# One layer of a conditioned hybrid decoder: both heads of a pair scored in one step, the mask added to the gate row, SSD decay on ScalarE, the later modulation sums on VectorE

## The chip, the core and the metric

The kernel runs on one core of one Trainium2 chip. A core has TensorE (PE in the profile; PEld is its weight load), VectorE (DVE), ScalarE (ACT), GpSimd (POOL) and SyncE (SP), which here issues every DMA. The metric is device time in microseconds (us), the median of the timed runs.

## The reference, cut to what matters

One layer, batch 1, 1024 tokens, width 1024, all in float32:

```
mod = silu(c) @ w_ada + b_ada -> sh1, sc1, g1, sh2, sc2, g2
h   = x * (1 + sc1) + sh1 ;  proj = h @ w_in -> z | xBC | dt | q | k | v | f
SSD (16 heads of 64, chunks of 128):  conv + SiLU on xBC;  a_cs = cumsum(dt * A)
    scores[l,s] = (C B^T)[l,s] * exp(a_cs[l] - a_cs[s]) for s <= l, else 0;  y = scores @ x + carried state
FoX (16 heads of 64, blocks of 128 queries):  logit[t,s] = q_t . k_s / 8 + cum[t] - cum[s], s <= t
    softmax over s, times v          (cum: running sum of log forget gates)
y = concat @ w_out;  x = LN(alpha x + (1+g1) y)
h = x * (1 + sc2) + sh2;  x = LN(alpha x + (1+g2) (relu(h W1)^2 W2))
```

## The kernel before, in words

All large products are done as three matmuls of a high and a low part (`split`, L72 to L88: hi = rounded to fp32r, lo = rest; products hi·hi, hi·lo, lo·hi). Activations lie transposed, features on partitions and tokens on columns. The stages, in the order of time:

1. **h tiles** (L148): for each of 8 blocks of 128 features the sums for sc1 and sh1 (`ada_sum`, L128: 512 KB of `w_ada`, a GpSimd product, a VectorE reduction over k, then a matmul with ones), then h = x·(1+sc1)+sh1 and its split.
2. **SSD**, head pair by head pair (`ssd`, L380). Per pair the 24 matmuls of each half of a projection (`conv_tile`, `z_tile`), the chunk states, and the decay scores: GpSimd subtracts the pair's column of `cs` from the broadcast row `arow` (L414), VectorE takes the minimum with 0 (L415), ScalarE the Exp (L416), VectorE the product with C·B (L417); eight matmuls per head follow, all of one head, then all of the other. Their weights `xc` have 64 columns, so each head writes one half of the 128 output partitions: the profile calls the shape 128*64 (rows*columns of the array). They are true f32 products, of two MATMUL records each.
3. **Attention** in units (pair, g, head), g = 0 to 3, each of two blocks of 128 queries (`probs`, L490). q and k of a head are stored stacked, hi on its 64 partitions and lo on the other 64 (L468 to L475); `swap` (L523) makes a copy of q with the halves exchanged by DMA. So two matmuls that use all 128 rows give the four products, and a third, of bf16 constants, adds the causal mask in PSUM. VectorE adds the gate row `cum` and takes the maximum (L515), ScalarE does the Exp, GpSimd the division. `weigh` transposes the probabilities and multiplies with v.
4. Between the units a generator `fill` puts in the projections of the next pair and then the first half of the output projection; PIECES says how many pieces go where. `ada_some` puts in the later modulation sums (sc2, sh2, g2, g1: `ada_rest`, 32 steps), and `w2_sums` (L170, 14 calls in the attention loop) differences of blocks of the second MLP weight, on GpSimd through tile `w_b`.
5. Second half of the output projection, layer norm, and the two MLP products in a seven-product (Strassen) form.

The order on each engine is not the order of the text: the tile scheduler lists the instructions by a timing model of its own. A load may start as soon as its buffer is free, so `w2_sums`, written in the attention loop, stands far earlier in the program that is built. `with after(x)` keeps a load behind instruction x.

PSUM has tags `mm` (1 bank), `o` (1), `t` (2 buffers of one bank) and `S` (2 buffers of two banks).

Of the kernel before, what the change touches and what calls it, by code (L numbers as in the profile page):

```python
# [27 lines left out]
NEG = -1.0e30  # L28
# [4 lines left out]
def layer_kernel(ctx, tc, x, xT, cols, rows3, w_ada, b_ada, w_in, w_dtf, w_out, ln_rows, w1, w2, out):  # L33
# [59 lines left out]
    identb = cst.tile([P, P], BF16, name="identb")  # L93
    nc.vector.tensor_copy(identb, identf)
# [33 lines left out]
    def ada_sum(sec, j, tag, name):  # L128
# [4 lines left out]
        red = sb.tile([P, P], F32, name="ada_red", tag="q2", bufs=4)  # L133
# [39 lines left out]
    def w2_sums():  # L173
# [4 lines left out]
        load(t, w2r[:, :, n, :].rearrange("p i (h c) -> p i h c", h=2))  # L178
# [9 lines left out]
    def ada_rest(sec, j):  # L188
        red = ada_sum(sec, j, "raw", "r")
        yield  # L190
        pst = PT("mm", "adar_ps", (P, P))
        if sec in (G1, G2):
            mm(pst, ones, red, True, True)
            if j == 0:
                gsum[sec] = dr.tile([P, 1024], F32, name=f"grow{sec}")
            g = sb.tile([P, P], F32, name="ada_g", tag="q2", bufs=4)
            nc.vector.tensor_copy(g, pst)
            load(gsum[sec][:, j * P:(j + 1) * P], g)
        else:
            mm(pst[:, 0:1], red, ones[:, 0:1], True, True)  # L200
            nc.vector.tensor_tensor(mod_t[:, sec, j:j + 1], pst[:, 0:1], b_t[:, sec * 8 + j:sec * 8 + j + 1], op=ALU.add)

    rest = [(s, j) for s in (SC2, SH2, G2, G1) for j in range(8)]

    pend = []

    def ada_some(n):
        for g in pend:
            next(g, None)
        pend.clear()  # L210
        for _ in range(min(n, len(rest))):
            g = ada_rest(*rest.pop(0))
            next(g)
            pend.append(g)
# [104 lines left out]
    def forget_rows():
# [6 lines left out]
        row_form(16)  # L326
# [54 lines left out]
    def ssd(p, xs, z):  # L381
# [27 lines left out]
        ydg = PT("S", "s2_ps", (P, 8, P))  # L409
        for h in range(2):  # L410
# [37 lines left out]
    def qkv(p, st):  # L448
# [3 lines left out]
        for n, idx, scale in (("q", KI + p, 0.125), ("k", VI + p, 1.0), ("v", None, None)):  # L452
            w, _ = ws[-1]
            if idx is not None:
                ws.append(w_prep(w_in[idx]))
                marks["w"] = ws[-1][1]
                st[n] = ts = [R4("qk", f"{n}_st") for _ in range(2)]
# [3 lines left out]
            for half in range(2):  # L461
# [93 lines left out]
    def finish(p, g, o, yT):  # L555
# [687 lines left out]
```

## Time and profile before

| | |
|---|---|
| median of 3 runs | 1744.4 us (1743.99 to 1746.87) |
| the profiled execution | 1748.06 us, of which the span of the instructions is 1746.3 us |
| mean granted TensorE clock | 0.976 |
| busy: PE, PEld, DVE, ACT, POOL | 1661.9, 1382.3, 1290.3, 704.5, 889.5 us |
| chain that ended last | PE 70%, DVE 17%, issue 4%, POOL 3%, DMA 3%, ACT 3% |

The ends of matmuls in the profile are modelled: a record of 0.39 us may be followed by the next after 0.23 us, and only the distance from start to start says what a matmul costs in a stream. A row such as `x38` holds 38 merged instructions: first start, then the time to the end of the last. "f32" in a matmul row is the width of the words; it doesn't tell fp32r from float32.

### The profile page before, as it was taken

How to read it: one execution, taken by the hardware profiler on the slowest of the kernel's cores; microseconds unless marked ns; L12 is line 12 of the kernel's file. 1: busy time of each engine (PE TensorE's matmuls, PEld its weight loads, DVE VectorE, ACT ScalarE, POOL GpSimd, SP SyncE). 2: the span in 40 equal slices, each digit the busy share in tenths (PEclk: the TensorE clock that was granted, in tenths of full speed). 3: DMA queues.
4: the chain of work that ended last, by engine and by line, in shares of the span. 5: the costliest groups of instructions: out<-in, count | busy, mean ns of one | idle time of the engine just before them, and what ended most of it. 6: DMA issues, size and time to landing. Idle time of an engine off the chain costs nothing.

```text
span 1746.3 us, 22839 instructions
## 1 busy us (share of the span) xinstructions
PE 1661.9 (95%) x8316; PEld 1382.3 (79%) x8316; DVE 1290.3 (74%) x1914; ACT 704.5 (40%) x1189; POOL 889.5 (51%) x686
## 2 busy tenths in 40 slices
PE   7878899999999999999999999799999999999996
PEld 6667688888888888888778887688888878888885
DVE  6889878886777777776776478986767855746668
ACT  3235332322444544553665434633333334344322
POOL 5859863533544444442442445566656624704535
PEclk8989999999999999999999999899999999999998
DMA  9467764422223323222333744044434596666512
GB/s 373 149 210 258 246 217 137 151 79 77 96 84 115 103 85 117 90 66 63 109 123 113 237 157 169 37 164 144 145 137 160 175 342 208 248 243 205 193 37 96
DMA packets 112032, 268.72 MB, mean 154 GB/s; under 512 B 10128, under 2 KB 37008, under 8 KB 111920
## 3 DMA queue, kind: packets, MB, share of 16 engines
q1 hardware_dynamic: 111920, 267.27, 44.6%
q8 instruction: 65, 1.06, 0.2%
q14 instruction: 47, 0.39, 0.1%
HBM read 194.22 MB, written 64.62 MB: 148 GB/s over the span
## 4 chain that ended last, share of the span: by engine, by line
PE 70%; DVE 17%; issue 4%; POOL 3%; DMA 3%; ACT 3%; SPq 0%; DVEq 0%; ACTq 0%; POOLq 0%
PE mm_ps L62 25%; PE f_ps L953 15%; PE s_ps L1069 9%; PE y_ps L1069 7%; PE s_ps L62 6%; PE o_ps L62 4%; PE t_ps L542 3%; DVE conv_a L345 2%; DVE ada_red L134 1%; DVE w_hl L85 1%; POOL w_b L181 1%; DMA w_b<-in_w_dram 1%; DMA raw_w<-in_w_dram 1%; DVE h_hl L85 1%; DVE probs L515 1%
## 5 line engine op out<-in xcount | busy, mean ns | idle before, releaser
L62 PE MATMUL mm_ps<-h_hl,w_hl 128*128 128x512 f32 x2016 | 504.7, 400 | 8.1 <-DVE w_hl L85 5.2
L62 PEld LDWEIGHTS mm_ps<-h_hl,w_hl 128*128 128x128 f32 x2016 | 372.6, 191 | 83.6 <-DVE w_hl L85 7.1
L85 DVE TENSOR_TENSOR w_op<-raw_w,w_op 128x512 fp32r<-128x512 f32 (+1 forms) x149 | 188.2, 1268 | 22.9 <-ACT w_op L81 22.4
L953 PE MATMUL f_ps<-h_s,w_op 128*128 128x512 f32 x768 | 183.3, 393 | 6.2 <-ACT h_s L81 3.0
L520 POOL TENSOR_SCALAR probs<-probs,m 128x128 f32<-128x128 f32 (+7 forms) x128 | 101.9, 800 | 157.0 <-DVE m L519 137.7
L953 PEld LDWEIGHTS f_ps<-h_s,w_op 128*128 128x128 f32 x768 | 145.6, 190 | 38.0 <-ACT h_s L81 3.4
L81 ACT CAST w_op<-raw_w 128x512 fp32r<-128x512 f32 (+1 forms) x149 | 114.7, 775 | 100.7 <-PE f_ps L953 52.9
L1069 PE MATMUL s_ps<-w_op,a_op 128*128 128x512 f32 x672 | 153.7, 390 | 1.4 <-DVE a_op L85 1.1
L1069 PEld LDWEIGHTS s_ps<-w_op,a_op 128*128 128x128 f32 x672 | 125.9, 188 | 28.7 <-DVE a_op L85 1.6
L85 DVE TENSOR_TENSOR a_op<-a_ld,a_op 128x1024 fp32r<-128x1024 f32 x53 | 75.3, 1422 | 97.3 <-ACT a_op L81 97.3
L132 POOL TENSOR_TENSOR raw_ada<-raw_ada,c_act 128x1024 f32<-128x1024 f32 x44 | 94.8, 2162 | 99.0 <-DMA raw_ada<-in_w_ada_dram 82.4
L953 PE MATMUL f_ps<-h_hl,w_op 128*128 128x512 f32 x576 | 136.8, 389 | 0.0
L518 ACT ACTIVATE probs<-probs,m 128x128 f32<-128x128 f32 (+7 forms) x128 | 99.3, 776 | 90.9 <-DVE m L517 79.0
L953 PEld LDWEIGHTS f_ps<-h_hl,w_op 128*128 128x128 f32 x576 | 108.0, 188 | 22.4
L515 DVE CUSTOM_DVE_ANT_0 probs<-s_ps,cumrow 128x128 f32<-128x128 f32 (+7 forms) x128 | 95.1, 753 | 37.0 <-PE s_ps L62 23.2
L544 ACT CAST pt_hl<-t_ps 128x512 fp32r<-128x512 f32 (+1 forms) x160 | 84.6, 541 | 87.9 <-PE t_ps L542 85.6
L81 ACT CAST a_op<-a_ld 128x1024 fp32r<-128x1024 f32 x53 | 55.7, 1054 | 159.7 <-PE s_ps L1069 85.1
L545 DVE TENSOR_TENSOR pt_hl<-t_ps,pt_hl 128x512 fp32r<-128x512 f32 (+1 forms) x160 | 99.7, 632 | 21.2 <-ACT pt_hl L544 19.9
L62 PE MATMUL o_ps<-pt_hl,v_s 128*128 128x256 f32 (+1 forms) x640 | 111.8, 297 | 3.5 <-DVE m L517 1.5
L1069 PE MATMUL y_ps<-w_op,a_op 128*128 128x512 f32 x504 | 114.7, 389 | 0.0
L85 DVE TENSOR_TENSOR w_hl<-raw_w,w_hl 128x512 fp32r<-128x512 f32 x88 | 81.7, 937 | 39.5 <-POOL w_hl L79 39.3
L1069 PEld LDWEIGHTS y_ps<-w_op,a_op 128*128 128x128 f32 x504 | 94.6, 188 | 19.6
(255 smaller groups left out, 3214.1 us busy)
## 6 DMA issues: line engine op xcount, KB each, us to landing
raw_w<-in_w_dram SPq DMA_DIRECT2D x57, 512.0 KB, 4.1
a_ld<-ad SPq DMA_DIRECT2D x49, 512.0 KB, 4.4
raw_ada<-in_w_ada_dram SPq DMA_DIRECT2D x48, 512.0 KB, 4.0
raw_w<-in_w_in_dram SPq DMA_DIRECT2D x44, 512.0 KB, 3.8
w_b<-in_w_dram SPq DMA_DIRECT2D x14, 1024.0 KB, 7.5
w2t<-w_b SPq DMA_DIRECT2D x14, 1024.0 KB, 5.1
ad<-a_s SPq DMA_DIRECT2D x28, 512.0 KB, 3.3
raw_w<-w2t SPq DMA_DIRECT2D x28, 512.0 KB, 4.9
```

What stands on the lines that cost most here:

```text
L62: nc.tensor.matmul(o, l, r, start=start, stop=stop)
L81: nc.scalar.copy(hi, raw)
L85: eng.tensor_tensor(lo, raw, hi.bitcast(F32), op=ALU.subtract)
L132: nc.gpsimd.tensor_tensor(raw, raw, c_act.unsqueeze(2).broadcast_to([P, KT, P]), op=ALU.mult)
L515: nc.vector.tensor_tensor_reduce(out=pt, in0=sp[:, :W], in1=cum[:, :W], op0=ALU.add, op1=ALU.max, scale=1.0, scalar=-3.0e38, accum_out=m[: ...
L518: nc.scalar.activation(pt, pt, AF.Exp, bias=m[:, 1:2], scale=1.0, accum_out=m[:, 2:3])
L520: nc.gpsimd.tensor_scalar(pt, pt, m[:, 3:4], 1.0, op0=ALU.mult, op1=ALU.mult)
L542: nc.tensor.transpose(tp[:, at:at + P], pts[ti][:, s * P:(s + 1) * P], identf)
L544: nc.scalar.copy(hl[:, 0, :n], tp[:, :n])
L545: nc.vector.tensor_tensor(hl[:, 1, :n], tp[:, :n], hl[:, 0, :n].bitcast(F32), op=ALU.subtract)
L953: nc.tensor.matmul(o, l, r, start=first and k == 0 and m == 0, stop=last and k == 3 and m == 2, skip_group_check=True)
L1069: nc.tensor.matmul(banks[j], ahl[a_][:, n, js], whl[w_][:, n, :], start=first and d == 0 and n == 0 and m == 0, stop=last and d == ND - 1 ...
```

## The change

- **Scores of attention.** A unit is now (pair, g) with both heads. q and k of a pair are split into hi and lo tiles with one head on partitions 0 to 63 and the other on 64 to 127; `probs` does three products (hi·hi, hi·lo, lo·hi) per head on 64 rows of the array, written so that the heads alternate. The swapped copy, its DMAs and the stacking on GpSimd and VectorE are gone. g now runs 3, 2, 1, 0.
- **Mask.** No bf16 matmul: GpSimd adds the mask to the 128 diagonal columns of the gate row in place. The sign of q·k and of the row is turned, so that the minimum is taken, which serves the Exp directly as bias; the small negation on VectorE is gone.
- **SSD decay.** Subtraction and minimum become eight ScalarE Relus of 128 columns per head, with the column of `cs` as bias; the Exp takes scale -1. The eight matmuls of the two heads alternate.
- **Later modulation sums.** `w_adb` is laid out so that a load brings two k blocks of 512 columns; VectorE does one multiply-add over 512 columns per k block, in 32 steps of two, in place of GpSimd's product and VectorE's reduction. A matmul follows every four steps. g1 and g2 are kept as one row.
- **w2_sums** moves to the SSD loop, two calls per pair, and its load waits for a projection's weight load.

```diff
-    def ada_rest(sec, j):
-        red = ada_sum(sec, j, "raw", "r")
+    def ada_rest(sec, hg):
+        red = sb.tile([P, 512], F32, name="ada_sum", tag="ada", bufs=1)
+        for kp in range(4):
+            raw = T4("raw", "raw_adb", shape=(P, 2, 512))
+            load(raw, w_adb[((sec - 2) * 2 + hg) * 4 + kp])
+            for i in range(2):
+                c = c_act[:, 2 * kp + i:2 * kp + i + 1]
+                if kp == 0 and i == 0:
+                    nc.vector.tensor_scalar(red, raw[:, i, :], c, None, op0=ALU.mult)
+                else:
+                    nc.vector.scalar_tensor_tensor(red, raw[:, i, :], c, red, op0=ALU.mult, op1=ALU.add)
+            yield
...
-        load(t, w2r[:, :, n, :].rearrange("p i (h c) -> p i h c", h=2))
+        with after(marks["w"]):
+            load(t, w2r[:, :, n, :].rearrange("p i (h c) -> p i h c", h=2))
...
-            nc.gpsimd.tensor_tensor(sc, ar, cs[:, :, h0 + h:h0 + h + 1].broadcast_to([P, 8, P]), op=ALU.subtract)
-            nc.vector.tensor_scalar(sc, sc, 0.0, None, op0=ALU.min)
-            nc.scalar.activation(sc, sc, AF.Exp)
+            for b in range(8):
+                nc.scalar.activation(sc[:, b, :], ar[:, b, :], AF.Relu, bias=cs[:, b, h0 + h:h0 + h + 1], scale=-1.0)
+            nc.scalar.activation(sc, sc, AF.Exp, scale=-1.0)
             nc.vector.tensor_tensor(sc, sc, CBM[g], op=ALU.mult)
-            for b in range(8):
-                mm(ydg[h * 64:h * 64 + 64, b, :], xc[:, b, h, :], sc[:, b, :], True, True)
+            scs.append(sc)
+        for b in range(8):
+            for h in range(2):
+                mm(ydg[h * 64:h * 64 + 64, b, :], xc[:, b, h, :], scs[h][:, b, :], True, True)
...
-        wn = w_prep(w_in[XI + p + 1])[0]
+        wn, marks["w"] = w_prep(w_in[XI + p + 1])
         ssd(p, *xz[p])
+        for _ in range(2):
+            w2_sums()
...
-                    e = sm.tile([P, 512], F32, name="qk_e", tag="o_half", bufs=2)
-                    nc.scalar.activation(e, o, AF.Copy, scale=scale)
-                    for h in range(2):
...
-                        nc.gpsimd.tensor_scalar(t[mine, hs], e[mine, :], 1.0, 1.0, op0=ALU.mult, op1=ALU.mult)
-                        nc.vector.tensor_tensor(t[other, hs], e[mine, :], t[mine, hs].bitcast(F32), op=ALU.subtract)
+                    split(o, st[n][0][:, hs], st[n][1][:, hs], "act", scale=scale)
...
-                mm(sp[:, s0:s1], q1[:, tb * P:(tb + 1) * P], k[:, s0:s1], True, False)
-                mm(sp[:, s0:s1], q2[:, i * P:(i + 1) * P], k[:, s0:s1], False, not last)
-                if last:
-                    mm(sp[:, tb * P:W], identb, maskb, False, True)
+            for m, (a, b) in enumerate(((qh, kh), (qh, kl), (ql, kh))):
+                for h in range(2):
+                    hp = slice(h * 64, h * 64 + 64)
+                    mm(u["sp"][h][:, at + s0:at + s1], a[hp, tb * P:(tb + 1) * P], b[hp, s0:s1], m == 0, m == 2)
+        for h in range(2):
+            sp, pt, cum = u["sp"][h][:, at:at + W], u["pt"][h][:, at:at + W], cums[u["p"]][h]
+            nc.gpsimd.tensor_tensor(cum[:, tb * P:W], cum[:, tb * P:W], maskf, op=ALU.add)
...
-            if g in (1, 3) or p == 7:
-                ada_some(2)
-            if g in (0, 2) and p < 7:
-                w2_sums()
+        if g in (0, 2) or p == 7:
+            ada_some(2)
```

**Where the instructions go.** GpSimd in the h tiles: `raw_ada` are the products of stage 1, `w_hl` splits of projection weights, `w_b` the sums of the second MLP weight. Before:

```order
L132 TENSOR_TENSOR raw_ada<-raw_ada,c_act 128x1024 x8
L79 TENSOR_SCALAR w_hl<-raw_w 128x512
L181 TENSOR_TENSOR w_b<-w_b 128x512 x2
L132 TENSOR_TENSOR raw_ada<-raw_ada,c_act 128x1024
L79 TENSOR_SCALAR w_hl<-raw_w 128x512
L181 TENSOR_TENSOR w_b<-w_b 128x512 x2
L132 TENSOR_TENSOR raw_ada<-raw_ada,c_act 128x1024
L181 TENSOR_TENSOR w_b<-w_b 128x512 x2
```

The same place after the change:

```order
L128 TENSOR_TENSOR raw_ada<-raw_ada,c_act 128x1024 x8
L79 TENSOR_SCALAR w_hl<-raw_w 128x512
L128 TENSOR_TENSOR raw_ada<-raw_ada,c_act 128x1024 x2
L79 TENSOR_SCALAR w_hl<-raw_w 128x512
L128 TENSOR_TENSOR raw_ada<-raw_ada,c_act 128x1024 x2
L79 TENSOR_SCALAR w_hl<-raw_w 128x512 x3
L178 TENSOR_TENSOR w_b<-w_b 128x512 x2
L79 TENSOR_SCALAR w_hl<-raw_w 128x512
```

The `w_b` operations no longer stand between the products: 24 of the 56 stood ahead of the first pair's `xd` (L391), 9 do now.

PE in the SSD stage, the third pair's score matmuls (`scores_1385` and `scores_1400` are the two heads). Before:

```order
L62 MATMUL s2_ps_1354<-xd_1351,b_nat_545 128x128 x7
L62 MATMUL s2_ps_1382<-scores_1385,xc_1350 64x128 x8
L62 MATMUL s2_ps_1382<-scores_1400,xc_1350 64x128 x8
L62 MATMUL mm_ps_1522<-h_hl_298,w_hl_1492 128x512
L62 MATMUL adar_ps_1548<-ones_76,ada_red_1326 128x1
```

After (heads `scores_1424` and `scores_1437`):

```order
L62 MATMUL s2_ps_1393<-xd_1390,b_nat_541 128x128 x7
L62 MATMUL s2_ps_1421<-scores_1424,xc_1389 64x128
L62 MATMUL s2_ps_1421<-scores_1437,xc_1389 64x128
L62 MATMUL s2_ps_1421<-scores_1424,xc_1389 64x128
L62 MATMUL s2_ps_1421<-scores_1437,xc_1389 64x128
L62 MATMUL s2_ps_1421<-scores_1424,xc_1389 64x128
L62 MATMUL s2_ps_1421<-scores_1437,xc_1389 64x128
```

The heads alternate, through all sixteen.

PE in attention, first pair, query blocks of 384 and 512 columns. `s_ps_2876` and `s_ps_2923` are the PSUM tiles of the two heads, `q2` the swapped copy, `maskb` the mask. Before:

```order
L62 MATMUL s_ps_2923<-k_st_2675,q_st_2506 128x384
L62 MATMUL s_ps_2923<-k_st_2675,q2_2873 128x384
L62 LDWEIGHTS identb_74
L62 MATMUL s_ps_2923<-maskb_85,identb_74 128x128
L62 MATMUL s_ps_2876<-k_st_2674,q_st_2505 128x512
L62 MATMUL s_ps_2876<-k_st_2674,q2_2838 128x512
L62 LDWEIGHTS identb_74
L62 MATMUL s_ps_2876<-maskb_85,identb_74 128x128
```

After, again the first pair, query blocks of 384 and 256 columns; `s_ps_3194` and `s_ps_3195`, and `s_ps_3389` and its partner `s_ps_3390`, are the two heads' tiles:

```order
L62 MATMUL s_ps_3194<-k_hl_2821,q_hl_2655 128x384
L62 MATMUL s_ps_3195<-k_hl_2821,q_hl_2655 128x384
L62 MATMUL s_ps_3194<-k_hl_2822,q_hl_2655 128x384
L62 MATMUL s_ps_3195<-k_hl_2822,q_hl_2655 128x384
L62 MATMUL s_ps_3194<-k_hl_2821,q_hl_2656 128x384
L62 MATMUL s_ps_3195<-k_hl_2821,q_hl_2656 128x384
L62 MATMUL mm_ps_3425<-h_hl_294,w_hl_3122 128x512 x2
L540 MATMUL t_ps_3266<-identf_69,probs_3091 128x128
L540 MATMUL t_ps_3266<-identf_69,probs_3009 128x128 x2
L62 MATMUL s_ps_3389<-k_hl_2821,q_hl_2655 128x256
L62 MATMUL s_ps_3389<-k_hl_2822,q_hl_2655 128x256
L62 MATMUL s_ps_3389<-k_hl_2821,q_hl_2656 128x256
```

Two full matmuls and a mask per head have become three half ones. The heads alternate in some places and follow each other in others (the partner `s_ps_3390` comes four transposes later). The scheduler leaves the 576 half matmuls in 111 runs, with matmuls of the full array between them.

## Rows read from the trace of the kernel before

**Rows 1.** By stretch: length; busy PE, PEld, DVE, ACT, POOL (instructions); clock, DMA share, GB/s.
```profile
0.00:71.00 71.00, 57.23 (x232) 43.68 (x232) 51.38 (x60) 19.16 (x19) 43.26 (x33) 0.90 0.78 299
71.00:118.00 47.00, 34.67 (x149) 26.79 (x148) 44.19 (x42) 17.33 (x23) 32.25 (x22) 0.84 0.44 157
118.00:392.00 274.00, 255.86 (x1363) 214.97 (x1362) 229.97 (x271) 98.37 (x112) 170.10 (x105) 0.97 0.55 186
392.00:927.00 535.00, 523.64 (x3040) 443.81 (x3039) 389.33 (x920) 258.54 (x554) 228.04 (x263) 0.99 0.29 93
```

**Rows 2.** PE's waits, 0 to 118 us: us in total, times, longest.
```profile
PE ada_ps L62 <- DMA raw_ada<-in_w_ada_dram: 6.3, 1, 6.3
```

**Rows 3.** PE's waits, 118 to 392 us.
```profile
PE mm_ps L62 <- DVE w_hl L85: 4.8, 3, 2.6
```

**Rows 4.** Instructions on tile scores: duration ns min/median/max, first and last start, forms.
```profile
L62 PE MATMUL s_ps<-scores,xc x256: 272/273/323, 143.4 to 399.7; 128*64 128x128 f32 x128
L415 DVE TENSOR_SCALAR scores<-scores x16: 683/1761/2395, 136.2 to 350.8; 128x1024 f32<-128x1024 f32 x16
```

**Rows 5.** POOL by line and form, 0 to 118 us: busy us, mean ns, idle before.
```profile
L181 POOL TENSOR_TENSOR w_b<-w_b 128x512 f32<-128x512 f32 x24 | 37.7, 1586 | 16.5 <-DVE cbm L374 8.6 <-DMA w_b<-in_w_dram 7.8
```

**Rows 6.** POOL by line and form, 118 to 392 us.
```profile
L181 POOL TENSOR_TENSOR w_b<-w_b 128x512 f32<-128x512 f32 x32 | 54.7, 1715 | 10.2 <-DMA w_b<-in_w_dram 9.5
L414 POOL TENSOR_TENSOR scores<-arow,cs 128x1024 f32<-128x1024 f32 x16 | 38.1, 2393 | 9.0 <-PE s_ps L62 6.7 <-DVE rows L314 2.3
L132 POOL TENSOR_TENSOR raw_ada<-raw_ada,c_act 128x1024 f32<-128x1024 f32 x14 | 32.6, 2328 | 46.7 <-DMA raw_ada<-in_w_ada_dram 39.0 <-DVE prev L401 5.6 <-DVE mod_t L201 2.1
```

**Rows 7.** DVE by line and form, 118 to 392 us.
```profile
L134 DVE TENSOR_REDUCE ada_red<-raw_ada 128x128 f32<-128x1024 f32 x14 | 27.8, 1982 | 8.8 <-POOL raw_ada L132 8.8
L415 DVE TENSOR_SCALAR scores<-scores 128x1024 f32<-128x1024 f32 x16 | 24.0, 1506 | 1.8 <-POOL scores L414 1.8
```

**Rows 8.** Lines by form, whole span: a multiply-add of 512 columns, a ScalarE operation of 128.
```profile
L961 DVE SCALAR_TENSOR_TENSOR a_c<-a_c 128x512 f32<-128x512 f32 x64 | 69.4, 1102 | 0.1
L518 ACT ACTIVATE probs<-probs,m 128x128 f32<-128x128 f32 x16 | 6.4, 397 | 3.8 <-DVE m L517 3.6
```

**Rows 9.** PE timeline, short windows between 279 and 284 us: start us, us, instruction.
```profile
279.44 0.61 PE L62 MATMUL s_ps<-xd,b_nat 128*128 128x128 f32 x4
279.98 0.54 PE L62 MATMUL s_ps<-scores,xc 128*64 128x128 f32 x3
...
281.12 0.88 PE L62 MATMUL s_ps<-scores,xc 128*64 128x128 f32 x10
...
282.70 0.60 PE L62 MATMUL s_ps<-scores,xc 128*64 128x128 f32 x4
283.23 0.96 PE L62 MATMUL mm_ps<-h_hl,w_hl 128*128 128x512 f32 x3
```

**Rows 10.** PE timeline in attention, at 600 and at 609 us.
```profile
600.16 0.34 PE L62 MATMUL s_ps<-k_st,q 128*128 128x384 f32 x1
600.34 0.23 PE L62 MATMUL s_ps<-maskb,identb 128*128 128x128 bf16 x1
600.38 0.48 PE L62 MATMUL s_ps<-k_st,q_st 128*128 128x512 f32 x1
600.69 0.40 PE L62 MATMUL s_ps<-k_st,q 128*128 128x512 f32 x1
600.92 0.39 PE L62 MATMUL s_ps<-k_st,q_st 128*128 128x512 f32 x1
...
609.10 0.28 PE L62 MATMUL s_ps<-k_st,q_st 128*128 128x256 f32 x1
609.22 0.28 PE L62 MATMUL s_ps<-k_st,q 128*128 128x256 f32 x1
```

**Rows 11.** PE timeline in the h tiles: 32 of the 128 columns, then all.
```profile
57.35 0.61 PE L62 MATMUL mm_ps<-h_hl,dtf_hl 128*32 128x512 f32 x2
57.80 0.39 PE L62 MATMUL b_ps<-h_hl,w_hl 128*128 128x512 f32 x1
```

More of the change, by code (lines that the diff above doesn't have):

```diff
@@ L203, in layer_kernel @@
-    rest = [(s, j) for s in (SC2, SH2, G2, G1) for j in range(8)]
-    pend = []
-    def ada_some(n):
[L208 to L214, printed above, removed]
+            if hg == 0:
+                gsum[sec] = dr.tile([1, 1024], F32, name=f"grow{sec}")
+            nc.vector.tensor_copy(red[0:1, :], pst[0:1, :])
+            load(gsum[sec][:, hg * 512:hg * 512 + 512], red[0:1, :])
+        else:
+            pst = PT("mm", "adar_ps", (P, 4))
+            js = slice(hg * 4, hg * 4 + 4)
+            for j in range(4):
+                mm(pst[:, j:j + 1], red[:, j * P:(j + 1) * P], ones[:, 0:1], True, True)
+            nc.vector.tensor_tensor(mod_t[:, sec, js], pst, b_t[:, sec * 8 + hg * 4:sec * 8 + hg * 4 + 4], op=ALU.add)
@@ L217, in w_prep, with rest_all @@
+    def rest_all():
+        for sec in (SC2, SH2, G1, G2):
+            for hg in range(2):
+                yield from ada_rest(sec, hg)
+    rest = rest_all()
+    def ada_some(n):
+        for _ in range(n):
+            next(rest, None)
     def w_prep(src, hi_eng="pool", tag="w"):
@@ L305, in layer_kernel, with row_form @@
     rowd = dr.tile([32, T], F32, name="rowd")
-    def row_form(first):
+    def row_form(first, sign):
         rows = T4("misc", "rows")
@@ L456, in qkv @@
                 marks["w"] = ws[-1][1]
-                st[n] = ts = [R4("qk", f"{n}_st") for _ in range(2)]
+                st[n] = [R4("qk", f"{n}_hl") for _ in range(2)]
             else:
@@ L524, in swap, with prob_tiles @@
-    def swap(st, h, g):
-        q1 = st["q"][h]
-        t0 = 2 * g * P
-        q2 = sb.tile([P, 256], F32R, name="q2", tag="q2", bufs=4)
-        store(q2[0:64, :].bitcast(F32), q1[64:128, t0:t0 + 256].bitcast(F32))
-        store(q2[64:128, :].bitcast(F32), q1[0:64, t0:t0 + 256].bitcast(F32))
-        st.setdefault("q2", {})[h, g] = q2
+    steps = [0]
+    def prob_tiles():
+        steps[0] += 1
+        if steps[0] % 2:
+            t = T4("ex", "probs", shape=(P, 2, 1024))
+            return [t[:, 0, :], t[:, 1, :]]
+        return [T4("P", "probs") for _ in range(2)]
@@ new lines, in probs @@
+    def probs(u, i):
+        st, g = u["st"], u["g"]
+        tb = 2 * g + i
+        W = (tb + 1) * P
+        if g >= 2 or "sp" not in u:
+            u["sp"] = [PT("S", "s_ps", (P, 1024)) for _ in range(2)]
+            u["pt"] = prob_tiles()
+        at = 0 if g >= 2 else i * 512
+        (qh, ql), (kh, kl) = st["q"], st["k"]
+        for s0 in range(0, W, 512):
+            s1 = min(W, s0 + 512)
+            for m, (a, b) in enumerate(((qh, kh), (qh, kl), (ql, kh))):
[5 more added lines that the diff above has]
+            nc.gpsimd.tensor_tensor(cum[:, tb * P:W], cum[:, tb * P:W], maskf, op=ALU.add)
+            m = sm.tile([P, 4], F32, name="m", tag="m", bufs=6)
+            nc.vector.tensor_tensor_reduce(out=pt, in0=sp, in1=cum[:, :W], op0=ALU.add, op1=ALU.min, scale=1.0,
+                                           scalar=3.0e38, accum_out=m[:, 0:1])
+            nc.scalar.activation(pt, pt, AF.Exp, bias=m[:, 0:1], scale=-1.0, accum_out=m[:, 1:2])
+            nc.vector.reciprocal(m[:, 2:3], m[:, 1:2])
+            nc.gpsimd.tensor_scalar(pt, pt, m[:, 2:3], 1.0, op0=ALU.mult, op1=ALU.mult)
+            u["pts"][h][i] = pt
@@ L669, in out_ssm @@
                 part1["y"] = y_block(1, 0, "cum")
-    PIECES = {p: (0, 3, 1, 3) for p in range(NPAIR)}
-    PIECES[6] = (2, 2, 3, 1)
-    PIECES[7] = (0, 1, 2, 3)
+    PIECES = {p: {3: (1, 1), 2: (2, 2), 1: (2, 2), 0: (2, 2)} for p in range(NPAIR)}
+    PIECES[7] = {3: (1, 1), 2: (1, 1), 1: (2, 2), 0: (3, 3)}
     WO_STEP = 3
@@ L684, in layer_kernel, with start @@
             ada_some(1)
-    units = [(p, g, h) for p in range(NPAIR) for g in range(4) for h in range(2)]
+    units = [dict(p=p, g=g, st=sts[p], pts=[[None, None], [None, None]]) for p in range(NPAIR) for g in (3, 2, 1, 0)]
     cums = {}
     ys = {}
-    def start(unit):
-        p, g, h = unit
-        if g == 0 and h == 0:
+    def start(u, i):
+        p = u["p"]
+        if p not in cums:
+            cums[p] = []
             for hh in range(2):
```

119 lines of the change are left out of this document (35 added, 84 removed).

## The prediction

> **What bounds the kernel now.** I read first the busy time by stretch [rows 1], which cuts the span at the places where the change works: h tiles to 71 us, the start of SSD to 118, the SSD pairs to 392, attention to 927. The stretches behind run the same instructions before and after, and are taken as unchanged. The reader is to see two regimes. In attention PE is busy 523.6 of 535 us at a granted clock of 0.99: nothing is won there by relieving VectorE or GpSimd, and every PE instruction added or removed counts in full. Ahead of it PE is not full: it is idle 13.8, 12.3 and 18.1 us in the three stretches (stretch minus busy), 44 us together, of which 6.3 are the wait for the very first load [rows 2], and the mean clock granted is 0.90, 0.84 and 0.97. The clock has two levels, 1.2 and 2.4 GHz, so a mean of 0.84 is a third of the stretch at the lower one. VectorE is what PE waits for: it is busy 44.2 of 47 and 230.0 of 274 us, and the largest wait in the SSD pairs is for its part of a weight split [rows 3]. VectorE in turn is slowed by company: the same minimum over 1024 columns takes 0.68 us at best, 1.76 in the median and 2.40 at worst [rows 4], while GpSimd is busy 170 of 274 us [rows 1].
>
> Second I read the PE timeline start to start, because the modelled ends hide what a matmul costs in a stream. Lastly the orders of both programs, for what is queued where.
>
> **Part 1: work that leaves GpSimd and VectorE ahead of attention.**
> - `w2_sums`: before, 24 of its 56 GpSimd operations run before 118 us, 37.7 us [rows 5]; in the order of the changed program 9 stand ahead of the same point, so 15 × 1.59 = 24 us of GpSimd work leave the first two stretches, and the products of the h tiles no longer queue behind them. The sums aren't removed: these 15 run later, beside the SSD pairs. Their loads queue on SP behind a projection weight's load; nothing in this stage reads the results.
> - SSD decay: GpSimd loses 16 × 2.39 = 38.1 us [rows 6], VectorE 16 × 1.51 = 24.0 us [rows 7]. ScalarE gains 8 × 16 = 128 Relus of 128 columns. The nearest row is an Exp of 128 columns, 0.40 us [rows 8]: 51 us in eight bursts of 6.4 us, on an engine busy 98 of 274 us.
> - Modulation sums: GpSimd loses its products, 32.6 us in this stretch [rows 6], VectorE 14 reductions of 1.98 = 27.8 us [rows 7], and gains 14 steps of two multiply-adds of 512 columns: at 1.10 us each [rows 8] 30.9 us, and if the best case of a 1024-column operation, 0.68 us, is halved, 9.5 us. I take the upper end, since GpSimd stays busy beside it: 0 on balance. In attention VectorE isn't the bound, so the rest of the steps costs nothing there.
> - Together, in the SSD pairs: GpSimd 170 − 38 − 33 + 15 × 1.72 = 125 us; VectorE 230 − 24 + 3 = 209 us, and less stretching.
>
> What PE gets of this is bounded by its own idle time: 44 us less the 6 of the first load, so 38, and by its time at the lower clock, 0.10 × 71 + 0.16 × 47 + 0.03 × 274 = 23 us if all of it came back. The lower bound of both is nothing. I take half of the idle time that is not the first load, less a little for ScalarE's bursts, −17, and not quite half of the clock, −10. It is half because the chain (loads, split, conv, decay, product) keeps its dependencies, while its slow member gets faster.
>
> **Part 2: SSD score matmuls with alternating heads.** In a stream of one head they start every (0.60 − 0.27)/3 = 0.11 us. Around 281.3 us, where before the first head ends and the second begins, ten starts take 0.88 − 0.27 = 0.61 us, 0.07 apart instead of 0.11 [rows 4, 9]: two column halves of the array run side by side, and the second head's first matmul starts while the first head still has three to go. So PE looks ahead about four matmuls. With alternating heads all 32 records pair: from 3.25 us, start of the scores to start of what follows, to 16 × 0.11 + 0.25 = 2.0 us. −1.25 × 8 = −10 us, on the PE path; 0 if the following wait on VectorE ends no sooner.
>
> **Part 3: scores in attention.** Per head the blocks have 512 columns six times and 384, 256 and 128 twice each. Start to start a matmul costs 0.23 (512), 0.18 (384), 0.12 (256; I take 0.12 for 128 too), the mask 0.04 us [rows 10]. Before: 12 × 0.23 + 4 × 0.18 + 8 × 0.12 + 8 × 0.04 = 4.76 us per head, 76 for 16 heads. After: 18 × 0.23 + 6 × 0.18 + 12 × 0.12 = 6.66, 107 us, if the two heads don't overlap, +30. If row halves overlap as the column halves of rows 9 do, with a look-ahead of four, I count the 111 runs of the order one by one (in a run such as three of one head, then three of the other, all pair; a long run of one head pairs only in part): 66 us, −10. No row of this trace shows two row halves at once; I take −10, since the column halves are the nearest row.
>
> The Trainium skill ("TensorE: Matmul & The Clock Gate", Part 3) says that matmuls on different row groups of the array run concurrently, and gives 3.07 times for four of 32 rows; nothing here shows that for row halves, and the sum by it would be the −10.
>
> Against this stands a price for leaving the full array. Into the 64-column scores at 279.98 us: four of the shape before, 0.11 apart from 279.44, would let the next start at 279.88, it starts 0.10 later; the step to the second is 0.05 too long (0.27 for two steps instead of 0.22). Out of it: the next full matmul starts 0.20 after the last half one, 0.09 too late, and its successors take 0.57 for two steps instead of 0.46, 0.11 too much. Together 0.35 us per excursion [rows 9]. Against that, the shape of 32 columns gives way to the full one with no price at all: 0.45 us for two [rows 11]. So bounds of 0 and 0.35; I take 0.30, nearer to the row with half an array, because some runs begin where PE waits anyway. 111 × 0.30 = +33 us.
>
> The Trainium skill ("TensorEngine Tiling (Array Packing)", Key Properties) says that changing the tiling mode drains the array. The trace agrees for the 64-column shape, 0.35 us, and not for the 32-column one; by the rule without exception the sum would have +39 in place of +33.
>
> **Part 4: what else is new in attention.** The bank of a projection's half is now emptied by ScalarE's hi and then by VectorE's lo out of PSUM, where before one ScalarE copy freed it; and a step now fills both `S` buffers, so the next step's scores wait for two VectorE passes. GpSimd's mask addition queues behind the divisions, and VectorE's pass waits for it. PE has projections and transposes to fill in. Before, all its waits in this stretch make 11 us (535 − 523.6). I put +4 us, with 0 and +20 as ends (twice the present waits at most). Mask, stacking, swap DMAs and negation cost nothing on the path; their going is worth no more than the mask's 0.04 us counted above.
>
> **Sum.** −17 − 10 − 10 − 10 + 33 + 4 = −10 us. 1748 − 10 = 1738 us for the profiled execution; it stands 3.7 us above the median of 1744.4, so **1734 us**, 0.6% faster. Two large terms of opposite sign, −37 ahead of attention and +27 in it, nearly cancel.
>
> **The rivals.**
> 1. *Row halves don't run side by side, but the excursions cost.* Part 3 is then +30 + 33, the sum +30, 1774 us. For it: no row shows the overlap; the two 512-column streams are also four times as long as those in rows 9. Against it: column halves overlap in rows 9. This is the slower side: it decides as soon as less than half of the count's 40 us of overlap comes. Chance 0.20.
> 2. *Row halves run side by side and the excursions cost nothing.* For it rows 11, against it rows 9. Sum −43, 1701 us. 0.12.
> 3. *Neither: the half matmuls run as full ones, one by one, without a price.* Rows 11 would be the model. +30 + 0 + 4 − 37 = −3, 1741 us. 0.10.
> 4. *ScalarE takes VectorE's place in SSD.* The 16 Relus of a pair, 6.4 us in a row, stand in front of the copies that empty the projections' banks, where PE's next half is 24 × 0.23 = 5.5 us; the 27 us of idle time and clock then don't come back. Sum +17, 1761 us. Against it: 98 + 51 of some 250 us busy. 0.10.
>
> The forecast keeps 0.48.
>
> **How the numbers follow.** No change means within 0.2%, 3.5 us, which is about what a measurement of this kernel tells apart. The forecast, with some 14 us of spread from the halves taken in part 1, is faster in 0.68, the same in 0.15, slower in 0.17 of its cases; rival 1 nearly always slower, rival 2 faster, rival 3 faster in half, rival 4 slower. Weighted: faster 0.52, same 0.11, slower 0.37. The range runs from a little under rival 2 to rival 1: 1698 to 1776. The forecast's own is 1718 to 1754.
>
> **What would show it.** Right, step by step: the first `xd` of SSD well before its place now; score groups of 32 in SSD in 2.0 us instead of 3.3; in attention, two score matmuls of different heads starting within a few hundredths of a us, and the first full matmul after them late by a tenth. Attention (from its first probabilities to the last) longer by some 27 us, and its start some 37 us earlier. Wrong: half matmuls 0.23 us apart with alternating heads (rival 1 or 3); no late start behind them (rival 2 or 3); PE waiting for ScalarE in SSD (rival 4).

## The result, and where the time went

The changed kernel takes 1775.2 us in the median (1772.9 to 1779.6), the kernel before, measured beside it, 1744.2: ratio 1.0167, 95% interval 1.0153 to 1.0181. It is 31 us slower, where 10 us less were forecast. Its profiled execution took 1777.3 us, with a span of 1775.4.

The same view as [rows 1], of the changed kernel, cut at its own stages: h tiles, start of SSD, SSD pairs, attention up to the last `o_ps`, output projection. Columns as there.

```profile
0.00:58.00 58.00, 48.09 (x207) 37.99 (x208) 43.40 (x56) 18.17 (x17) 27.85 (x23) 0.94 0.67 258
58.00:110.00 52.00, 45.17 (x205) 35.08 (x204) 38.49 (x55) 19.72 (x27) 21.08 (x15) 0.93 0.44 168
110.00:403.00 293.00, 253.95 (x1406) 209.54 (x1405) 191.30 (x265) 129.03 (x236) 123.05 (x92) 0.94 0.56 193
403.00:982.00 579.00, 563.87 (x3169) 448.86 (x3168) 343.03 (x768) 271.27 (x576) 212.43 (x314) 0.99 0.21 73
982.00:1128.00 146.00, 140.91 (x653) 115.75 (x653) 101.61 (x127) 59.45 (x119) 73.36 (x54) 1.00 0.53 181
```

By the starts of matmuls (the last `o_ps` by its end), the 29 us between the two spans lie as follows (before, then after; all from the traces):

| place | before | after | difference | forecast |
|---|---|---|---|---|
| first `xd` of SSD at | 125.3 | 110.3 | −15 | earlier |
| first attention score at | 413.6 | 415.5 | +2 | −37 |
| from there to the last `o_ps` | 546.7 | 566.5 | +20 | +27 |
| from there to the first MLP matmul | 138.8 | 146.4 | +8 | 0 |
| from there to the end | 647.3 | 647.0 | 0 | 0 |

Up to 110 us the change does what was foretold. In the SSD pairs GpSimd's and VectorE's work also falls, to 123 us (125 foretold) and 191 us (209 foretold), from 170 and 230 in [rows 1]. Yet PE is idle 39 of 293 us there, where it was idle 18 of 274. So less work on the engines that PE waited for came with twice the idle time of PE. What it waits for now, as in [rows 3], from 110 to 415 us (us in total, times, longest):

```profile
PE mm_ps L62 <- POOL w_hl L79: 11.3, 4, 5.0
PE s_ps L392 <- DVE prev L403: 6.9, 2, 5.4
PE mm_ps L62 <- DVE w_hl L85: 6.8, 7, 1.6
PE s_ps L62 <- POOL xd L397: 4.9, 1, 4.9
```

The largest is a weight's split on GpSimd. GpSimd isn't busy then, as the timeline around 376 us shows (start us, us, engine, line, instruction; in brackets the idle time before it and what ended it):

```profile
374.52 0.95 PE L62 MATMUL adar_ps<-ones,ada_sum 128*128 128x1 f32 x8
...
375.50 0.16 DVE L209 TENSOR_TENSOR mod_t<-adar_ps,col 128x4 f32<-128x4 f32 x1 [2.90 <-PE adar_ps L62]
375.58 0.48 DVE L193 TENSOR_SCALAR ada_sum<-raw_adb,c_act 128x512 f32<-128x512 f32 x1
376.09 2.33 DVE L195 SCALAR_TENSOR_TENSOR ada_sum<-raw_adb,c_act,ada_sum 128x512 f32<-128x512 f32 x3
376.87 1.91 SPq L65 DMA_DIRECT2D raw_w<-in_w_in_dram  x2
380.17 1.20 POOL L79 TENSOR_SCALAR w_hl<-raw_w 128x512 fp32r<-128x512 f32 x2 [17.53 <-DMA raw_w<-in_w_in_dram]
...
380.84 1.22 PE L62 MATMUL mm_ps<-h_hl,w_hl 128*128 128x512 f32 x2 [4.45 <-POOL w_hl L79]
```

Read from below. PE lacks a weight for 4.45 us. GpSimd has been idle for 17.5 us because that weight's load is issued only at 376.87. It is issued then because both `raw` buffers hold modulation columns until VectorE has used them, and VectorE can't begin on them: the single accumulator (`tag="ada", bufs=1`) is in use until PE has summed the group before (eight matmuls from 374.52 on), and in VectorE's order the taking of that sum (375.50) stands ahead of the next group. PE's sums stand in PE's queue behind projections. So the next weight waits for PE, and PE for the weight. A like sequence stands at 225 to 235 us (sums from 225.1, next group from 226.1, weight's load issued at 227.5, PE idle for 5.0 us until 235.5). There the accumulator isn't alone: ahead of that load the sync queue stood at two row loads until ScalarE's Relus had freed their buffers, the second at 227.1.

In attention, the timeline of one short run of scores between projections, at 547 us:

```profile
547.21 0.39 PE L62 MATMUL mm_ps<-h_hl,w_hl 128*128 128x512 f32 x1
547.53 0.50 PE L62 MATMUL s_ps<-k_hl,q_hl 64*128 64x512 f32 x2
547.86 0.40 PE L62 MATMUL s_ps<-k_hl,q_hl 64*128 64x512 f32 x2
548.19 0.50 PE L62 MATMUL mm_ps<-h_hl,w_hl 128*128 128x512 f32 x1
```

Two half matmuls, one for each head, start together (x2 at 547.53 and at 547.86): the row halves do run side by side. But the steps are 0.32, 0.33 and 0.33 us where full matmuls of this width stand 0.23 apart [rows 10]: 0.10 us more going in, inside and coming out.

In SSD, 32 score matmuls of two alternating heads (foretold 2.0 us, before 3.25):

```profile
357.07 1.97 PE L62 MATMUL s_ps<-scores,xc 128*64 128x128 f32 x32
358.97 2.35 PE L62 MATMUL mm_ps<-h_hl,w_hl 128*128 128x512 f32 x9
```

They take 1.9 us from start to start.

### The profile page after: what moved, and what is told of

Same layout as the page of the kernel before. It is cut to its first block, busy times and chain, and to the rows that moved or that the text cites. A ratio compares the mean times of both kernels' runs of the same rounds, so it can differ in the third digit from the quotient of the medians.

```text
span 1775.4 us, 22614 instructions
## 1 busy us (share of the span) xinstructions
PE 1673.3 (94%) x8356; PEld 1359.1 (77%) x8356; DVE 1177.6 (66%) x1744; ACT 733.3 (41%) x1313; POOL 793.6 (45%) x702
## 4 chain that ended last, share of the span: by engine, by line
PE 62%; DVE 10%; DMA 10%; POOL 5%; ACT 4%; issue 2%; SPq 0%; DVEq 0%; ACTq 0%; POOLq 0%
PE mm_ps L62 20%; PE f_ps L940 13%; PE s_ps L1056 9%; PE s_ps L62 6%; PE y_ps L1056 6%; PE o_ps L62 4%; PE t_ps L540 3%; DMA raw_adb<-in_w_adb_dram 1%; POOL w_b L178 1%; DMA raw_o<-in_w_out_dram 1%; ACT scores L422 1%; DVE sq_red L609 1%; DMA yd<-ea 1%; DMA y_raw<-yd 1%; DVE ada_sum L195 1%
## 5 line engine op out<-in xcount | busy, mean ns | idle before, releaser
L79 POOL TENSOR_SCALAR w_hl<-raw_w 128x512 fp32r<-128x512 f32 x86 | 65.0, 758 | 246.5 <-PE mm_ps L62 112.3
L522 POOL TENSOR_TENSOR cumrow<-cumrow,maskf 128x128 f32<-128x128 f32 x128 | 62.1, 487 | 172.1 <-DVE m L524 149.7
L526 ACT ACTIVATE probs<-probs,m 128x896 f32<-128x896 f32 (+7 forms) x128 | 98.8, 774 | 59.0 <-DVE m L524 54.6
L528 POOL TENSOR_SCALAR probs<-probs,m 128x896 f32<-128x896 f32 (+7 forms) x128 | 100.3, 790 | 47.7 <-DVE m L527 45.9
L524 DVE CUSTOM_DVE_ANT_0 probs<-s_ps,cumrow 128x896 f32<-128x896 f32 (+7 forms) x128 | 92.9, 750 | 43.3 <-PE s_ps L62 41.5
```

The lines of the kernel that those rows point to most:

```text
L79: nc.gpsimd.tensor_scalar(hi, raw, 1.0, 1.0, op0=ALU.mult, op1=ALU.mult)
L522: nc.gpsimd.tensor_tensor(cum[:, tb * P:W], cum[:, tb * P:W], maskf, op=ALU.add)
L524: nc.vector.tensor_tensor_reduce(out=pt, in0=sp, in1=cum[:, :W], op0=ALU.add, op1=ALU.min, scale=1.0, scalar=3.0e38, accum_out=m[:, 0:1])
L526: nc.scalar.activation(pt, pt, AF.Exp, bias=m[:, 0:1], scale=-1.0, accum_out=m[:, 1:2])
L528: nc.gpsimd.tensor_scalar(pt, pt, m[:, 2:3], 1.0, op0=ALU.mult, op1=ALU.mult)
```

## The experiments

The first theory (A) was another than the one above: the sync queue stands at row loads whose buffers ScalarE's late Relus hold (61 us of its waits from 110 to 403 us), and weight loads stand behind them. Rivals: the w2 sums (B), the modulation loads in the weights' buffers (C), later sharpened to the single accumulator (D). Each ratio is to the kernel before, measured beside the run.

### Undoing parts of the change

**decay_back**

```diff
-            for b in range(8):
-                nc.scalar.activation(sc[:, b, :], ar[:, b, :], AF.Relu, bias=cs[:, b, h0 + h:h0 + h + 1], scale=-1.0)
-            nc.scalar.activation(sc, sc, AF.Exp, scale=-1.0)
+            nc.gpsimd.tensor_tensor(sc, ar, cs[:, :, h0 + h:h0 + h + 1].broadcast_to([P, 8, P]), op=ALU.subtract)
+            nc.vector.tensor_scalar(sc, sc, 0.0, None, op0=ALU.min)
+            nc.scalar.activation(sc, sc, AF.Exp)
```

> The changed kernel, with the SSD decay put back on GpSimd (subtraction) and VectorE (minimum); heads still alternate. Theory A: the SSD pairs lost 22 us against the forecast because ScalarE reaches its 16 Relus late, the row loads that wait for their buffers hold the sync queue, and weight loads stand behind them: then about 20 us faster than the changed kernel, 1755 us, with the last SSD score near 382 us instead of 402. Theory B (the w2 sums in the SSD pairs delay weights and GpSimd's splits): within 5 us of 1775. Theory C (modulation loads share the two buffers of the weight loads): within 5 us of 1775, or slower by up to 15, since GpSimd and VectorE get their 62 us back.

Measured 1778.2 us, ratio 1.0173 (1.0155 to 1.0192), the same as the changed kernel. Theory A falls as the main cause: with the decay off ScalarE the last SSD score ends at 400.6 instead of 402.5 us, not near 382. PE's longest wait is the one for the late weight, as at 376 us in the changed kernel; its load goes out right behind an accumulator step (the first of the three merged here ends at 374.24):

```profile
373.50 2.32 DVE L195 SCALAR_TENSOR_TENSOR ada_sum<-raw_adb,c_act,ada_sum 128x512 f32<-128x512 f32 x3
374.27 1.91 SPq L65 DMA_DIRECT2D raw_w<-in_w_in_dram  x2
...
378.63 0.79 PE L62 MATMUL mm_ps<-h_hl,w_hl 128*128 128x512 f32 x1 [6.49 <-POOL w_hl L79]
```

**w2_back**

```diff
-        with after(marks["w"]):
-            load(t, w2r[:, :, n, :].rearrange("p i (h c) -> p i h c", h=2))
+        load(t, w2r[:, :, n, :].rearrange("p i (h c) -> p i h c", h=2))
...
-        for _ in range(2):
-            w2_sums()
...
+        if g in (0, 2) and p < 7:
+            w2_sums()
```

> The changed kernel, with the w2 sums called from the attention loop and not held back behind a weight load, as in the kernel before. Theory B: the 22 us come back, the early 15 us go, net some 7 us faster, 1768 us. Theory A: only the early 15 us go, 1790 us. Theory C: like A, 1785 to 1790 us.

Measured 1790.2 us, ratio 1.0251 (1.0229 to 1.0274). The total is what A and C gave, but for another reason: the early 15 us did not go (the h tiles end at 58.1 us, as in the changed kernel). Attention started 15 us sooner (400.9 instead of 415.5; 6 of these are there at the first `xd`, at 103.8) and took 593 instead of 567 us. Here the sums share a tag with the probabilities, and all 56 run in attention. So the w2 sums do cost some 15 us ahead of attention, and would cost more in the new attention.

**ada_later**

```diff
         if p == 1:
             group_prep(1)
-        ada_some(2)
...
-            ada_some(1)
```

> The changed kernel without modulation steps in the SSD pairs (all 32 steps in attention). Theory C: some 15 to 20 us faster, 1757 us, since no weight load waits for a buffer that a modulation step holds, and the 7.9 us behind the modulation matmuls go. Theory A: no more than 5 us faster; theory B: the same. Under each, attention may get 0 to 5 us longer by the steps that it takes over.

Measured 1768.6 us, ratio 1.0113 (1.0095 to 1.0131). Attention starts at 393.4 instead of 415.5 us: 22 us go with the modulation steps, what the steps themselves take included. 14 of them come back behind, since from there to the MLP it takes 727 instead of 713 us; steps now run beside the last pair, where two waits of PE of 0.8 us stand right behind their sums.

**ada_back** puts back `ada_rest` and `ada_some` of the kernel before (128 columns each, in the four `q2` buffers), called from the new places:

```diff
-    def ada_rest(sec, hg):
-        red = sb.tile([P, 512], F32, name="ada_sum", tag="ada", bufs=1)
...
+    def ada_rest(sec, j):
+        red = ada_sum(sec, j, "raw", "r")
...
+    rest = [(s, j) for s in (SC2, SH2, G2, G1) for j in range(8)]
```

> The changed kernel with the modulation sums of the kernel before (128 columns, product on GpSimd, reduction on VectorE, 32 accumulators in four buffers), called from the new places. Theory D: the waits of D go, GpSimd and VectorE get 30 us of work each back in the SSD pairs: 5 to 20 us faster than 1775. Theory C: the loads are as many and as large and share the same buffers: 1775 or slower, up to 1790.

Measured 1801.5 us, ratio 1.0329 (1.0310 to 1.0348). Neither theory gave that much. Attention starts 5 us sooner than in the changed kernel but takes 597 us, with GpSimd busy 238 us there against 211. PE's largest wait in it is for VectorE's sum of the output halves, 9.8 us. So the old form costs the new attention 30 us, and this run doesn't separate C from D.

### The accumulator by itself

**ada_two**

```diff
-        red = sb.tile([P, 512], F32, name="ada_sum", tag="ada", bufs=1)
+        red = sm.tile([P, 512], F32, name="ada_sum", tag="o_half", bufs=2)
```

> The changed kernel with two accumulators for the modulation sums instead of one (in two buffers that nothing else uses before the MLP). Theory D: at the end of a group of 512 columns the next step's first product waits until PE has summed the accumulator, behind projections in its queue; both buffers of the weight loads are then held by modulation loads, the next weight comes late, and PE waits (5.3 us at 230, 5.6 and 5.3 at 300 to 308, 4.7 at 376 us): then 10 to 20 us faster than 1775, and those waits are gone. Theory C (the modulation loads take turns with the weight loads in two buffers, whatever ends them): within 5 us of 1775.

Measured 1757.5 us, ratio 1.0063 (1.0051 to 1.0076): 18 us faster than the changed kernel. By stretch, then PE's largest waits from 110 to 388 us:

```profile
110.00:375.00 265.00, 248.86 (x1405) 206.24 (x1405) 183.22 (x263) 132.04 (x238) 125.21 (x92) 0.98 0.62 214
375.00:959.00 584.00, 572.20 (x3171) 454.89 (x3171) 345.30 (x771) 271.85 (x577) 215.31 (x314) 0.99 0.21 73
```

```profile
PE mm_ps L62 <- DVE w_hl L85: 5.5, 5, 1.6
PE s_ps L62 <- DVE prev L407: 3.9, 3, 2.2
PE mm_ps L62 <- POOL w_hl L79: 2.4, 2, 1.3
```

The SSD pairs take 265 instead of 293 us with the same loads, the same buffers for them and the same multiply-adds; PE is idle 16 us in place of 39, and the granted clock rises from 0.94 to 0.98. The four waits of about 5 us are gone, and VectorE begins a group long before PE has summed the one before, here 22 us:

```profile
199.99 1.51 DVE L193 TENSOR_SCALAR ada_sum<-raw_adb,c_act 128x512 f32<-128x512 f32 x1
222.31 0.95 PE L62 MATMUL adar_ps<-ones,ada_sum 128*128 128x1 f32 x8
```

That is D, and C falls as a cause by itself. One reservation: the program's order was set anew with two accumulators, so the run shows them together with the order that follows. Two of the four waits, those that begin at 300 and 308 us, had no accumulator in their chain: VectorE stood 10.7 us behind ScalarE's Exp. That they are gone is the new order's doing.

**two_decay_back** is decay_back on two accumulators.

> Two accumulators, with the SSD decay on GpSimd and VectorE. If the decay on ScalarE is worth what the prediction gave it (GpSimd 38 us, VectorE 24 us of relief) and the wait for the accumulator hid it: 8 to 15 us slower than 1757.5. If ScalarE's bursts cost as much as the relief gives: within 4 us of 1757.5. If theory A is right once the accumulator no longer decides: 5 to 10 us faster.

Measured 1775.1 us, ratio 1.0164 (1.0148 to 1.0181), 17.6 us slower than ada_two, a little more than the 8 to 15 expected, and all of it ahead of attention, which starts at 408.5 us and takes 570 us as in ada_two. The SSD pairs of it, then PE's waits from 110 to 408 us:

```profile
110.00:395.00 285.00, 253.27 (x1405) 210.38 (x1403) 217.04 (x277) 98.44 (x112) 165.84 (x108) 0.95 0.59 200
```

```profile
PE s_ps L62 <- DVE prev L407: 8.3, 3, 4.2
PE s_ps L62 <- POOL xd L397: 7.2, 3, 6.1
```

The decay on ScalarE is worth 18 us with two accumulators and nothing with one. Without it GpSimd and VectorE have 41 and 34 us more to do, and PE waits for both.

### Alternating heads in SSD

**before_alt** and **two_in_turn** add and remove the alternation on either side:

```diff
-            for b in range(8):
-                mm(ydg[h * 64:h * 64 + 64, b, :], xc[:, b, h, :], sc[:, b, :], True, True)
+            scs.append(sc)
+        for b in range(8):
+            for h in range(2):
+                mm(ydg[h * 64:h * 64 + 64, b, :], xc[:, b, h, :], scs[h][:, b, :], True, True)
```

> The kernel before, with the SSD score matmuls alternating between the two heads and nothing else. By the prediction's own term 10 us faster, 1734 us; the changed kernel's trace gives 13 us less behind score matmuls (28.5 to 15.6 us), 1731 us. If the following wait for VectorE ends no sooner: 0, 1744 us.

> Two accumulators, with the SSD score matmuls of one head after the other. If alternating is worth its 13 us of PE time once nothing else holds PE: 10 to 13 us slower than 1757.5. If the next step waits for VectorE all the same, as in the kernel before with alternating heads alone: within 4 us.

Measured 1745.9 us, ratio 0.9993 (0.9983 to 1.0002), for the first; 1758.5 us, ratio 1.0063 (1.0050 to 1.0077), for the second, where ada_two has the same ratio. The score steps did change, from 28.5 to 16.2 us in before_alt and from 15.9 to 26.1 in two_in_turn, and the end did not. PE's largest wait in before_alt, 118 to 392 us, against [rows 3]:

```profile
PE mm_ps L62 <- DVE w_hl L85: 13.8, 5, 8.5
```

PE does its scores sooner and waits 9 us longer for VectorE's next split.

### The w2 sums by themselves

**before_w2** puts the w2 edit alone into the kernel before:

```diff
-        load(t, w2r[:, :, n, :].rearrange("p i (h c) -> p i h c", h=2))
+        with after(marks["w"]):
+            load(t, w2r[:, :, n, :].rearrange("p i (h c) -> p i h c", h=2))
...
-        wn = w_prep(w_in[XI + p + 1])[0]
+        wn, marks["w"] = w_prep(w_in[XI + p + 1])
         ssd(p, *xz[p])
+        for _ in range(2):
+            w2_sums()
...
-            if g in (0, 2) and p < 7:
-                w2_sums()
```

> The kernel before with one part of the change alone: the w2 sums called from the SSD pairs, each load behind a weight's load. If the 15 us gained up to 110 us come from these 15 sums leaving GpSimd there, and SSD hides them: 1730 us, 0.9% faster. If SSD pays them back in full: 1745 us.

Measured 1750.3 us, ratio 1.0022 (1.0012 to 1.0031). The h tiles end at 58.2 us and the first `xd` comes 11 us sooner, but the first attention score is at 416.5 us, 3 later than before: SSD pays all of it back. GpSimd still has the decay and the products there, which may be why; no run tests that.

### The price of the half array

**scores_in_turn**

```diff
-            for m, (a, b) in enumerate(((qh, kh), (qh, kl), (ql, kh))):
-                for h in range(2):
-                    hp = slice(h * 64, h * 64 + 64)
+            for h in range(2):
+                hp = slice(h * 64, h * 64 + 64)
+                for m, (a, b) in enumerate(((qh, kh), (qh, kl), (ql, kh))):
```

> The changed kernel, with the attention scores of one head after the other (three matmuls each) instead of alternating. If alternating row halves run side by side: the 288 pairs that start within a few hundredths of a us pair only where head changes, and attention is 20 to 45 us longer, 1795 to 1820 us. If PE looks ahead far enough to pair them all the same (the count of the prediction with a look-ahead of four): 1775 to 1785 us. If halves gain nothing by running together: 1775 us.

Measured 1796.4 us, ratio 1.0285 (1.0271 to 1.0299), 21 us slower than the changed kernel; attention takes 586 us instead of 567. PE's order has 129 runs of half matmuls here instead of 111; by the price measured below, an estimate, 18 more are 8 of the 21 us. The other 13 are then overlap that is lost, and some is left, since pairs still form where the head changes.

**full_first** and **full_within** (on two accumulators). The extra matmul of full_within begins a sum in a bank in which another is under way, so the scores of 48 blocks are not the reference's in it; kind and number of the instructions are those of full_first.

```diff
+                if m == 0 and s0 == 0 and W % 512:
+                    nc.tensor.matmul(u["sp"][0][:, at + W:at + W + P], qh[:, tb * P:(tb + 1) * P], kh[:, 0:P],
+                                     start=True, stop=True, skip_group_check=True)
                 for h in range(2):
```

In full_within the condition is `m == 1 and s1 == W and W % 512`, and nothing else differs.

> Two accumulators, and 48 extra full-array matmuls of 128 columns (into score columns that nobody reads), each ahead of a block's half matmuls. Runs of half matmuls in PE's order: 116, as before (114). The control of the next kernel: 48 matmuls of 0.06 to 0.11 us, 3 to 5 us slower than 1757.5, 1761 us, under each theory.

> The same 48 full-array matmuls, each after the first pair of a block's last chunk instead of ahead of it: 155 runs of half matmuls instead of 116. If a run costs the 0.30 us of the prediction: 39 times 0.30, 12 us slower than the control. If as much as the sum over the changed kernel's steps leaves for it (about 0.5 us): 19 us slower. If leaving and entering the full array is free and the longer attention has another cause: within 3 us of the control.

Measured 1756.3 us, ratio 1.0057 (1.0041 to 1.0074), and 1774.3 us, ratio 1.0156 (1.0143 to 1.0170). Each kernel from its last SSD score to its last `o_ps`, first full_first, then full_within:

```profile
379.00:963.00 584.00, 568.61 (x3219) 455.53 (x3220) 348.33 (x771) 272.18 (x576) 211.82 (x314) 0.99 0.21 73
```

```profile
377.00:978.00 601.00, 586.02 (x3221) 459.82 (x3220) 348.38 (x770) 273.25 (x577) 211.49 (x314) 1.00 0.21 71
```

17 us in that stretch and 18 in the medians for 39 more runs of half matmuls: 0.43 to 0.46 us each. The control costs nothing, where 3 to 5 us were expected; why isn't shown, and PE's waits don't take its 48 matmuls up, since PE is idle 15 us in this stretch against 12 in ada_two. The price contains the pairs that a split run no longer forms, as in any short run.

### The output stage, and the better kernel

**two_pieces**

```diff
+    PIECES[6] = {3: (1, 1), 2: (2, 2), 1: (2, 2), 0: (3, 3)}
```

> Two accumulators, and 16 instead of 14 pieces of projection beside the seventh pair's units, as in the kernel before, so that the output projection starts earlier. If the 8 us that the output stage got longer come from its late start (first root-mean-square sum 878.8 us before, 905.6 after): 3 to 8 us faster than with two accumulators alone, 1752 us. If they come from loads or from the bank that ScalarE empties: 1757 us.

Measured 1767.8 us, ratio 1.0124 (1.0109 to 1.0138): 10 us slower than ada_two and outside both expectations, though the first root-mean-square sum comes 6 us sooner. Attention takes 580 us, 9 more than in ada_two, and the output stage 151, 3 more. An earlier start doesn't shorten the output stage.

**early_only** is the kernel before with the changed code ahead of attention, and its modulation sums in groups of 256 columns, for which two accumulators fit beside the old attention once `o_2` has one buffer in place of two and `q2` three in place of four (not in this cut):

```diff
+        red = sb.tile([P, 256], F32, name="ada_sum", tag="ada", bufs=2)
+        for kp in range(2):
+            raw = T4("raw", "raw_adb", shape=(P, 4, 256))
...
-            ot = sm.tile([P, 256], F32, name="o_half", tag="o_2", bufs=2)
+            ot = sm.tile([P, 256], F32, name="o_half", tag="o_2", bufs=1)
```

> The kernel before in attention and behind it; ahead of attention the changed one: w2 sums in the SSD pairs, decay on ScalarE, heads alternating, modulation sums on VectorE, these in groups of 256 columns with two accumulators. Theory D with the scores' price: SSD ends 25 us earlier than before (as with two accumulators, 388 against 413 us) and attention costs what it did, so 1722 us, 1.4% faster than before; the 8 us behind attention don't appear. Rival (the gain ahead of attention comes back as waits in attention, because the work moved out of it or into it meets the loads there): 1740 to 1750 us.

Measured 1733.6 us, ratio 0.9925 (0.9912 to 0.9938), the fastest of all. It lies between the 1722 expected and the rival's 1740: of the 25 us ahead of attention 12 came. Attention starts at 401.4 us (413.6 before), takes 546.4 us and the output stage 139.2, both as before. PE's two largest waits from 110 to 400 us end with VectorE's taking of the modulation sums, and in attention PE waits 7.6 us for VectorE's softmax columns:

```profile
PE s_ps L62 <- DVE mod_t L213: 5.8, 2, 3.5
PE mm_ps L62 <- DVE mod_t L213: 3.8, 2, 2.0
...
PE s_ps L62 <- DVE m L530: 7.6, 6, 2.9
```

This settles that the 20 to 24 us in attention and the 8 behind it come with the new attention code. What takes the other 13 us ahead of attention was not tested.

## Why the prediction was wrong

**The step that failed** is in part 1, "Modulation sums": "0 on balance". It compared the durations of old and new multiply-adds (the new ones took 0.75 us in the median, below the 1.10 that was taken) and never asked how many sums may be under way. Before, the 32 sums had four small buffers; after, one accumulator, whose next use waits for a PE instruction behind projections while the weights' buffers are held. Cost: 18 us in the medians, 27 us at the start of attention (415.5 against 388.2 with two accumulators). With two, attention starts 25 us earlier than before; the forecast's terms for it were −17 −10 −10 = −37. Even then the kernel is 0.6% slower than before, not 0.6% faster: the 10 us of the alternation don't come, and the output stage takes 8 us that stood in no term.

**The other early terms.** Moving the w2 sums gives 11 of the early 15 us by itself and nothing in the end (before_w2). The decay on ScalarE fits, as foretold: 18 us with two accumulators. Rival 4, ScalarE in the place of VectorE, falls with it, and its 1761 us had the right direction for the wrong reason. So had rival 1: its 1774 us is what was measured, but by luck, since the halves do run side by side. Alternation: the −10 was right as PE time (1.9 us a group against 2.0 foretold) and wrong on the path; the condition written beside it ("0 if the following wait on VectorE ends no sooner") is what happened.

**Attention** had the right mechanism, and two sizes that were wrong in opposite ways. The row halves overlap, as the count assumed from column halves, and the excursions cost: 0.43 to 0.46 us where 0.30 was taken and 0.35 was the upper bound, some 15 us more for 111 runs. Against that the old scores were counted too low: from start to next start they take 88.7 us with their masks and PE's waits, where 76 were counted. The new ones take 90.0, and the transposes, behind which many runs begin, 14.3 more (71.2 against 56.9). So +27 came as +20, and +24 with two accumulators; that it came so near is partly luck. The Trainium skill ("TensorE: Matmul & The Clock Gate", Part 3) says that row groups run concurrently; starts 3 ns apart at 547.53 agree. It also says ("TensorEngine Tiling (Array Packing)", Key Properties) that changing the mode drains the array; here a run of halves costs about 0.4 us, which agrees. By an estimate the price takes back what the overlap gives: 111 runs times 0.44 are 49 us, against the 41 that the forecast's count gave the overlap (107 to 66).

**The output stage** was taken as unchanged and got 8 us longer. Most of that is work that changed sides: in the traces 190 of the output projection's 768 matmuls stand ahead of the last `o_ps`, where before, and in early_only, 210 did. 20 matmuls at 0.23 us are 4.6 us, and PE's waits in the stage are 5.0 us against 2.8. So on equal work attention got nearer 25 us longer than 20, and the output stage 3. In two_pieces only 193 stand ahead, so its two pieces didn't undo this.

## What to carry to other kernels

When work is regrouped into larger pieces, count the buffers that each piece holds and for how long, and follow who frees them: a single accumulator that another engine must read ties that engine's queue to every load that shares a buffer with its inputs. Busy times came out as forecast here while PE's idle time doubled. And one such loop hides the other terms: the decay was worth nothing in front of it and 18 us behind it, so an edit that shows nothing alone is to be tried again once the wait is gone.

## What the runs showed of the hardware

- Two matmuls of 64 rows by 512 columns on the two row halves start 3 ns apart, and two such pairs take 0.66 us to the next start, four full ones 0.91.
- Going from full matmuls of 512 columns to halves the first start is 0.09 us late (0.318 against 0.227), after a transpose of 128 columns 0.17 (0.202 against 0.028), the next step inside is 0.10 too long, and the next full matmul after a pair again 0.10 late. These steps make 0.3 to 0.4 us; the whole price of a further run is 0.43 to 0.46 us in full_within, lost pairs included.
- 48 additional full matmuls of 128 columns beside the scores cost no measurable time (1756.3 against 1757.5 us).
